# Two hybrid decoder layers on one core: the feed forward's low weight halves made by an accumulating transfer

## The chip, the core and the metric

The kernel runs on one core of a Trainium2 chip. The metric is device time in microseconds of one execution; lower is better. The kernel before takes 1782.17 us, the median of three runs (1781.2 to 1785.3).

## What is computed

Two post-norm decoder layers over 512 tokens of width 1024. Each merges three causal mixers (pooling, a state-space layer called S5, sparse attention) and ends with a squared-ReLU feed forward of width 4096. Only the last lines matter for the change:

```python
D_FF = 4 * D_MODEL
...
    x = layer_norm(ALPHA * x + merged @ w_out, ln1_g, ln1_b)
    h = jnp.square(jax.nn.relu(x @ w_ff1)) @ w_ff2
    return layer_norm(ALPHA * x + h, ln2_g, ln2_b)
```

`w_ff1` is 1024 x 4096 and `w_ff2` 4096 x 1024, in float32, for each of the two layers: 32 tiles of 128x1024 (512 KB) each, so 64 weight tiles a layer.

## The kernel before

**Split products.** Every matrix product is made of three on TensorE (PE) in the reduced format float32r. An operand x is split into hi (x rounded to float32r) and lo (x minus hi, again in float32r), and `mm3_` (L92 to L101) issues hi·hi (L98), hi·lo (L99) and lo·hi (L100) into one PSUM bank. In the first product of the feed forward the weights stand first, so their low half is read by L100 (`mm<-xh,wl`); in the second product they stand second, and it is read by L99 (`t<-wl,hi_a`).

**Loading a weight tile.** `wload` (L69 to L86) does it: a transfer on SyncE's queue (SP) brings 128x1024 float32 into a staging tile `wst` (L79, two buffers), ScalarE (ACT) rounds it into `wh` (L82, four buffers), and L85 subtracts to give `wl` (four buffers). The subtraction is on VectorE (DVE), or on GpSimd (POOL) where the tile comes from a pool of its own or `share` says so. A staging tile is free again when both of its readers, L82 and L85, are done, so SP's next load waits for them.

**The feed forward.** `feed_forward` (L1225) runs eight stages c. Stage c issues `up(c + 1)`, four tiles of the first weights, each used by 24 matmuls in a row, then `down(c)`, two halves of two tiles of the second weights. In a half four token blocks use both tiles, 48 matmuls. `up(0)` uses four tiles that were loaded in the stage before, and `down(7)` has code of its own. So in each layer 28 + 28 = 56 tiles go through the two calls that the change touches (L1100 and L1136).

**What else runs there.** In layer 0, POOL has other work during the feed forward: `ln_affine` (L215, lines L222 and L223, 16 instructions) applies scale and offset to the residual, and `s5_ahead` (L533) makes four sets of operands for the next layer's S5 (L461 to L464, L514 to L528, L542), which SP writes out (L547). At c = 2, `feed_forward` also loads four tiles of the next layer's input projection (L1249, `in_win`, tiles 1254 to 1265 in the rows of the order below), whose subtraction is on POOL. In layer 1, POOL has only `ln_affine`.

The tile framework sets the order of instructions on each engine when the program is built; each engine then takes its own in that order.

Of the kernel before, what the change touches and what calls it, by code (L numbers as in the profile page):

```python
# [12 lines left out]
AF = mybir.ActivationFunctionType  # L13
OP = mybir.AluOpType
# [12 lines left out]
class Kern:  # L27
# [38 lines left out]
        self.nc.scalar.activation(hi, src, AF.Copy, scale=scale)  # L66
        self.nc.vector.scalar_tensor_tensor(lo, src, scale, hi.bitcast(F32), op0=OP.mult, op1=OP.subtract)

    def wload(self, ap, pool=None):  # L69

        n = ap.shape[1]
        with ExitStack() as order:
            if self.held:
                self.held -= 1
                for ins in self.behind:
                    order.enter_context(self.tc.issue_after(ins))
            order.enter_context(self.tc.high_priority())
            st = self.t(self.wp, [128, n], F32, "wst", 2)
            self.loaded = self.nc.sync.dma_start(st, ap).ins  # L79
            wh = self.t(pool or self.wp, [128, n], R, "wh", 4)  # L80
            wl = self.t(pool or self.wp, [128, n], R, "wl", 4)
            self.nc.scalar.copy(wh, st)  # L82
            self.n_w += 1
            e = self.nc.gpsimd if pool or self.wpool or self.share and self.n_w % self.share == 0 else self.nc.vector
            e.tensor_tensor(wl, st, wh.bitcast(F32), OP.subtract)  # L85
        return wh, wl  # L86
# [1006 lines left out]
    def ffn(self, i, xs, p0):  # L1093

        nc, v = self.nc, self.nc.vector

        def up(c):
            hs = []
            for m in range(4):
                ps = p0[m] if c == 0 else self.xw([self.wload(self.A["wf1"][i, 4 * c + m])])[0]  # L1100
                h = self.t(self.mt, [128, 512], F32, "mt")
                nc.scalar.activation(h, ps, AF.Relu)  # L1102
                v.tensor_tensor(h, h, h, OP.mult)  # L1103
                hh, hl = self.pair("ab"[c % 2])
                self.hi_lo(hh, hl, h)
                hs.append((hh, hl))
            return hs

        def part(hs, ws, tb, half, c):
            ps = self.psum("mm" if c == 7 else "s" if tb % 2 else "t")  # L1110
            s = slice(tb * 128, (tb + 1) * 128)
            terms = []
            for k in range(4):
                hh, hl = hs[k]
                wh, wl = ws[2 * half + k // 2]
                cc = slice((k % 2) * 512, (k % 2 + 1) * 512)
                terms.append(((hh[:, s], hl[:, s]), (wh[:, cc], wl[:, cc])))
            self.mm3(ps, terms)
            r = xs[tb][:, half * 512:(half + 1) * 512]
            v.tensor_tensor(r, r, ps, OP.add)  # L1120

        def blocks(hs, ws, post):
            for tb in range(4):
                for half in range(2):
                    part(hs, ws, tb, half, 7)
                    if half:
                        post(tb)
                    yield

        def down(c, hs, post):  # L1130
            W = self.A["wf2"]
            if c < 7:
                for half in range(2):
                    ws = [None] * 4
                    for kp in range(2):
                        ws[2 * half + kp] = self.wload(W[i, c, half, kp])  # L1136
                    for tb in range(4):
                        part(hs, ws, tb, half, c)
            else:
                ws = [self.wload(W[i, c, half, kp]) for half in range(2) for kp in range(2)]  # L1140
                return blocks(hs, ws, post)

        return up, down

    def run(self):
# [214 lines left out]
```

## Time and profile before

| what | value |
|---|---|
| median of three runs | 1782.17 us |
| the profiled execution | 1785.11 us |
| its span, first to last instruction | 1783.3 us |
| PE busy | 94% of the span |
| DVE, ACT, POOL busy | 63%, 40%, 31% |
| HBM traffic over the span | 102 GB/s |

A profile row of a group gives line, engine, operation, tile out<-in, shapes and count, then busy time in us, mean ns of one, and idle time before it with what ended that. A row of a window gives each engine's busy time with its number of instructions, the granted clock of TensorE (1.00 is the higher of its two levels, 0.50 the lower), the share of the 16 transfer engines and GB/s.

### The profile page before, as it was taken

The numbers are of one execution on the slowest core, as the hardware profiler recorded it, in microseconds if no ns is written. First come the engines' busy times: TensorE is split into PE (matmuls) and PEld (weight loads), VectorE is DVE, ScalarE is ACT, GpSimd is POOL, SyncE is SP. The second block draws the span as 40 slices with busy tenths as digits, with TensorE's granted clock in tenths as the row PEclk, the third lists the DMA queues.
The fourth block names the chain that finished last, engine by engine and source line by source line (L and its number), as shares of the span: only waits on it lengthen the run. The fifth ranks groups of instructions, "written<-read, shape, count | busy, mean of one in ns | idle before, by whom it ended". The sixth has DMA issues, their size and how long they took to land.

```text
span 1783.3 us, 22543 instructions
## 1 busy us (share of the span) xinstructions
PE 1676.9 (94%) x8356; PEld 1402.0 (79%) x8356; DVE 1129.7 (63%) x2167; ACT 711.3 (40%) x1245; POOL 552.4 (31%) x640
## 2 busy tenths in 40 slices
PE   3959999999999998999998899999999999999996
PEld 2957887887779886888887788878787888888885
DVE  8797568676578654544476555866756784444447
ACT  2444336666534332233232433556664342332221
POOL 4993321322114999400024233132212060000002
PEclk9979999999999998999999999999999999999998
DMA  5313251111351243443316433311124133233331
GB/s 192 116 37 95 85 185 60 60 48 63 93 176 41 87 160 115 166 140 96 115 54 224 137 111 113 125 53 60 60 83 149 65 118 95 94 95 95 99 102 59
DMA packets 64334, 183.69 MB, mean 103 GB/s; under 512 B 12256, under 2 KB 21216, under 8 KB 63200
## 3 DMA queue, kind: packets, MB, share of 16 engines
q1 hardware_dynamic: 61632, 176.88, 30.5%
q10 hardware_dynamic: 2592, 5.38, 0.9%
q8 instruction: 65, 1.06, 0.2%
q14 instruction: 45, 0.37, 0.1%
HBM read 164.93 MB, written 17.30 MB: 102 GB/s over the span
## 4 chain that ended last, share of the span: by engine, by line
PE 71%; DVE 12%; POOL 10%; DMA 3%; ACT 2%; issue 1%; SPq 0%; DVEq 0%; ACTq 0%; POOLq 0%
PE mm L98 15%; PE mm L99 14%; PE mm L100 14%; PE s L99 3%; PE s L98 3%; PE s L100 3%; PE o L834 3%; PE t L98 2%; PE t L99 2%; PE t L100 2%; PE t L929 2%; DVE wl L85 1%; PE s L901 1%; ACT wh L82 1%; POOL ct L461 1%
## 5 line engine op out<-in xcount | busy, mean ns | idle before, releaser
L82 ACT CAST wh<-wst 128x1024 fp32r<-128x1024 f32 (+1 forms) x260 | 270.3, 1042 | 548.4 <-PE s L100 205.3
L85 DVE TENSOR_TENSOR wl<-wst,wh 128x1024 fp32r<-128x1024 f32 (+2 forms) x208 | 276.7, 1332 | 251.6 <-ACT wh L82 251.3
L98 PE MATMUL mm<-xh,wh 128*128 128x512 f32 (+1 forms) x1088 | 429.7, 395 | 6.1 <-ACT wh L82 4.9
L100 PE MATMUL mm<-xh,wl 128*128 128x512 f32 (+1 forms) x1088 | 419.3, 385 | 5.7 <-DVE wl L85 5.7
L99 PE MATMUL mm<-xl,wh 128*128 128x512 f32 (+1 forms) x1088 | 418.8, 385 | 0.0
L100 PEld LDWEIGHTS mm<-xh,wl 128*128 128x128 f32 x1088 | 205.1, 188 | 48.2 <-DVE wl L85 6.8
L98 PEld LDWEIGHTS mm<-xh,wh 128*128 128x128 f32 x1088 | 205.6, 189 | 44.5 <-ACT wh L82 5.4
L99 PEld LDWEIGHTS mm<-xl,wh 128*128 128x128 f32 x1088 | 205.9, 189 | 33.6
L85 POOL TENSOR_TENSOR wl<-wst,wh 128x1024 fp32r<-128x1024 f32 x52 | 132.1, 2543 | 243.1 <-ACT wh L82 243.0
L193 POOL TENSOR_TENSOR xm<-xm,ln_g 128x512 f32<-128x512 f32 x9 | 12.2, 1367 | 321.4 <-ACT xm L192 321.4
L906 ACT ACTIVATE P<-P,mx 128x512 f32<-128x512 f32 (+3 forms) x128 | 71.3, 558 | 62.7 <-DVE mx L904 62.3
L904 DVE CUSTOM_DVE_ANT_0 P<-s,mask 128x512 f32<-128x512 f32 (+3 forms) x128 | 59.6, 484 | 46.3 <-PE s L901 38.7
L62 DVE TENSOR_TENSOR Pl<-t,Ph 128x384 fp32r<-128x384 f32 (+1 forms) x96 | 57.3, 597 | 36.2 <-ACT Ph L61 36.0
L1120 DVE TENSOR_TENSOR xm<-xm,t 128x512 f32<-128x512 f32 x56 | 38.4, 686 | 56.0 <-PE t L100 53.2
L222 POOL TENSOR_TENSOR xm<-xm,hi_a 128x512 f32<-128x512 f32 x8 | 12.6, 1581 | 182.7 <-PE t L238 182.7
L222 POOL TENSOR_TENSOR xm<-xm,ln_g 128x512 f32<-128x512 f32 x16 | 30.1, 1884 | 121.8 <-PE t L238 121.8
L1103 DVE TENSOR_TENSOR mt<-mt 128x512 f32<-128x512 f32 x64 | 57.1, 892 | 14.8 <-ACT mt L1102 14.8
L1120 DVE TENSOR_TENSOR xm<-xm,s 128x512 f32<-128x512 f32 x56 | 38.2, 682 | 39.8 <-PE s L100 39.8
L913 POOL TENSOR_SCALAR P<-P,sm,gate 128x128 f32<-128x128 f32 x32 | 15.4, 480 | 153.1 <-DVE sm L908 153.1
L98 PE MATMUL t<-wh,hi_a 128*128 128x512 f32 x128 | 50.7, 396 | 8.9 <-ACT wh L82 8.9
L61 ACT CAST Ph<-t 128x384 fp32r<-128x384 f32 (+1 forms) x96 | 48.0, 505 | 26.9 <-PE t L929 26.8
L98 PE MATMUL mm<-hi_a,wh 128*128 128x512 f32 x132 | 54.9, 416 | 2.5 <-DVE lo_a L318 2.5
(406 smaller groups left out, 3839.8 us busy)
## 6 DMA issues: line engine op xcount, KB each, us to landing
wst<-in_wf_dram SPq DMA_DIRECT2D x128, 512.0 KB, 3.5
wst<-in_win_dram SPq DMA_DIRECT2D x80, 512.0 KB, 3.3
wst<-in_wup_dram SPq DMA_DIRECT2D x24, 512.0 KB, 3.5
wst<-in_wout_dram SPq DMA_DIRECT2D x16, 512.0 KB, 4.2
s5d<-zwe SPq DMA_DIRECT2D x4, 1664.0 KB, 8.6
zwe<-s5d SPq DMA_DIRECT2D x4, 1664.0 KB, 8.4
xd<-xm SPq DMA_DIRECT2D x8, 512.0 KB, 4.8
w<-in_w_dram SPq DMA_DIRECT2D x8, 512.0 KB, 7.4
```

What stands on the lines that cost most here:

```text
L61: a = self.nc.scalar.copy(hi, src)
L62: b = self.nc.vector.tensor_tensor(lo, src, hi.bitcast(F32), OP.subtract)
L82: self.nc.scalar.copy(wh, st)
L85: e.tensor_tensor(wl, st, wh.bitcast(F32), OP.subtract)
L98: mm(out, ah, bh, start=first and i == 0, stop=False, **kw)
L99: mm(out, ah, bl, start=False, stop=False, **kw)
L100: mm(out, al, bh, start=False, stop=last and i == n - 1, **kw)
L834: mm = lambda o, a, b, **k: nc.tensor.matmul(o, a, b, skip_group_check=True, **k)
L904: v.tensor_tensor_reduce(out=p, in0=ss[qb], in1=self.mask[:, 384 - 128 * qb:512], scale=-1.0, scalar=3e38, op0=OP.add, op1=OP.min, accum_o ...
L906: nc.scalar.activation(p, p, AF.Exp, bias=mx[:, qb:qb + 1], scale=-1.0, accum_out=c)
L1103: v.tensor_tensor(h, h, h, OP.mult)
L1120: v.tensor_tensor(r, r, ps, OP.add)
```

## The change

For the 112 tiles of the two calls, `wl` is no longer a subtraction. ACT writes the negative of the rounded tile into `wl` (a second pass over `wst`), and POOL's queue issues a transfer that reads the same 512 KB from HBM again and adds it to `wl` in place.

```diff
-    def wload(self, ap, pool=None):
+    def wload(self, ap, pool=None, sums=False):
...
             self.nc.scalar.copy(wh, st)
+            if sums:
+                self.nc.scalar.activation(wl, st, AF.Copy, scale=-1.0)
+                self.nc.gpsimd.dma_start(wl, ap, accum_op=OP.add)
+                return wh, wl
             self.n_w += 1
...
-                ps = p0[m] if c == 0 else self.xw([self.wload(self.A["wf1"][i, 4 * c + m])])[0]
+                ps = p0[m] if c == 0 else self.xw([self.wload(self.A["wf1"][i, 4 * c + m], sums=True)])[0]
...
-                        ws[2 * half + kp] = self.wload(W[i, c, half, kp])
+                        ws[2 * half + kp] = self.wload(W[i, c, half, kp], sums=True)
```

In the new program the lines from the old L83 on stand four lines lower: L226 is the old L222, L89 the old L85. L84 is ACT's negative and L85 POOL's transfer.

Three places of POOL's order show where the transfers went. First, the start of layer 0's feed forward, where `ln_affine` runs. `xm` is the residual, `ln_g` and `ln_b` scale and offset. Before:

```order
L222 TENSOR_TENSOR xm_982_4864<-xm_982_4864,ln_g_968_4836 128x512
L223 TENSOR_TENSOR xm_982_4864<-xm_982_4864,ln_b_969_4837 128x512
L222 TENSOR_TENSOR xm_982_4864<-xm_982_4864,ln_g_968_4836 128x512
L223 TENSOR_TENSOR xm_982_4864<-xm_982_4864,ln_b_969_4837 128x512
L222 TENSOR_TENSOR xm_983_4866<-xm_983_4866,ln_g_968_4836 128x512
```

Now:

```order
L226 TENSOR_TENSOR xm_982_4864<-xm_982_4864,ln_g_968_4836 128x512
L85 DMA wl_1072_5571<-in_wf1_dram 128x1024
L227 TENSOR_TENSOR xm_982_4864<-xm_982_4864,ln_b_969_4837 128x512
L226 TENSOR_TENSOR xm_982_4864<-xm_982_4864,ln_g_968_4836 128x512
L85 DMA wl_1079_5610<-in_wf1_dram 128x1024
L227 TENSOR_TENSOR xm_982_4864<-xm_982_4864,ln_b_969_4837 128x512
L226 TENSOR_TENSOR xm_983_4866<-xm_983_4866,ln_g_968_4836 128x512
L85 DMA wl_1086_5649<-in_wf1_dram 128x1024
L85 DMA wl_1093_5688<-in_wf1_dram 128x1024
```

Between the first transfer, wl_1072, and the last instruction of `s5_ahead` (just behind wl_1365) POOL's order now holds 33 transfers. The second place is POOL around the four tiles of the next layer's input projection, from the last of their subtractions on. Before:

```order
L85 TENSOR_TENSOR wl_1265_6511<-wst_1263_6508,wh_1264_6510 128x1024
L461 TENSOR_TENSOR et0_1331_6859<-zwe0_1146_6011,s5_pr_36_229 128x8x2
L462 TENSOR_TENSOR et1_1332_6860<-zwe0_1146_6011,s5_pi_37_230 128x8x2
L461 TENSOR_TENSOR ct0_1398_7200<-Zc_1392_7186,s5_are2_34_223 128x256
L462 TENSOR_TENSOR ct1_1399_7201<-Zc_1392_7186,s5_aim2_35_224 128x256
```

Now:

```order
L89 TENSOR_TENSOR wl_1265_6531<-wst_1263_6528,wh_1264_6530 128x1024
L465 TENSOR_TENSOR et0_1331_6887<-zwe0_1146_6023,s5_pr_36_229 128x8x2
L466 TENSOR_TENSOR et1_1332_6888<-zwe0_1146_6023,s5_pi_37_230 128x8x2
L467 TENSOR_TENSOR Wc_1316_6833<-ct0_1323_6853,ct1_1324_6854 128x4x16
L468 TENSOR_TENSOR Wc_1316_6833<-ct0_1323_6853,ct1_1324_6854 128x4x16
L85 DMA wl_1268_6537<-in_wf2_dram 128x1024
L467 TENSOR_TENSOR zwe0_1146_6023<-et0_1331_6887,et1_1332_6888 128x4x2
L468 TENSOR_TENSOR zwe0_1146_6023<-et0_1331_6887,et1_1332_6888 128x4x2
```

The low half of the next feed-forward tile, wl_1268, was DVE's and is now issued by POOL behind that subtraction and four instructions of `s5_ahead`. The third place is a little later, still POOL, where one set of S5 operands is written (L528, the old L524):

```order
L85 DMA wl_1281_6614<-in_wf2_dram 128x1024
L467 TENSOR_TENSOR Wc_1316_6833<-ct0_1327_6865,ct1_1328_6866 128x4x16
L468 TENSOR_TENSOR Wc_1316_6833<-ct0_1327_6865,ct1_1328_6866 128x4x16
L467 TENSOR_TENSOR zwe0_1146_6023<-et0_1335_6899,et1_1336_6900 128x4x8
L468 TENSOR_TENSOR zwe0_1146_6023<-et0_1335_6899,et1_1336_6900 128x4x8
L528 TENSOR_SCALAR zwe0_1146_6023<-Wc_1316_6833 64x20x16 x4
L465 TENSOR_TENSOR ct0_1394_7224<-bc_1391_7220,s5_kre_29_127 128x8x16
L466 TENSOR_TENSOR ct1_1395_7225<-bc_1391_7220,s5_kim_30_128 128x8x16
L465 TENSOR_TENSOR et0_1337_6905<-zwe0_1146_6023,s5_pr_36_229 128x8x16
L466 TENSOR_TENSOR et1_1338_6906<-zwe0_1146_6023,s5_pi_37_230 128x8x16
L85 DMA wl_1288_6677<-in_wf1_dram 128x1024
```

Between two neighbouring transfers there stand twelve instructions here, since L528 stands for four.

## Rows read from the trace of the kernel before

**Rows 1.** The page's busy time of each engine.
```profile
PE 1676.9 (94%) x8356; PEld 1402.0 (79%) x8356; DVE 1129.7 (63%) x2167; ACT 711.3 (40%) x1245; POOL 552.4 (31%) x640
```
**Rows 2.** Windows: stretch, length, each engine's busy us, granted clock, DMA share, GB/s.
```profile
560.00:905.00 345.00, 336.11 (x1524) 279.62 (x1523) 184.22 (x213) 103.80 (x131) 171.83 (x273) 0.99 0.38 122
...
1430.00:1740.00 310.00, 309.99 (x1410) 258.31 (x1409) 158.24 (x176) 94.24 (x121) 23.70 (x14) 1.00 0.32 101
...
1600.00:1700.00 100.00, 100.00 (x443) 82.77 (x442) 45.86 (x55) 27.88 (x34) 0.00 (x0) 1.00 0.30 95
```
**Rows 3.** Waits of PE in layer 0's feed forward, 556 to 910 us.
```profile
PE t L98 <- ACT wh L82: 8.9, 1, 8.9
```
**Rows 4.** Windows around that wait (same columns).
```profile
680.00:685.00 5.00, 2.45 (x11) 1.69 (x9) 0.15 (x1) 1.54 (x2) 4.73 (x9) 1.00 0.62 210
685.00:690.00 5.00, 0.00 (x0) 0.00 (x0) 2.98 (x2) 1.66 (x2) 5.00 (x6) 0.54 0.32 105
690.00:695.00 5.00, 3.67 (x9) 2.85 (x10) 3.00 (x3) 2.62 (x4) 5.00 (x10) 0.50 0.54 139
695.00:700.00 5.00, 5.00 (x22) 4.09 (x21) 2.95 (x3) 1.53 (x2) 5.00 (x11) 0.93 0.56 175
```
**Rows 5.** Timeline of POOL there: start us, us, instruction.
```profile
677.53 4.75 POOL L85 TENSOR_TENSOR wl<-wst,wh 128x1024 fp32r<-128x1024 f32 x2
...
684.39 2.35 POOL L85 TENSOR_TENSOR wl<-wst,wh 128x1024 fp32r<-128x1024 f32 x1 [0.27 <-ACT wh L82]
...
688.02 2.84 POOL L85 TENSOR_TENSOR wl<-wst,wh 128x1024 fp32r<-128x1024 f32 x1
```
**Rows 6.** Timeline of SP's queue there.
```profile
653.01 0.42 SPq L547 DMA_DIRECT2D s5d<-zwe  x1
662.92 19.72 SPq L79 DMA_DIRECT2D wst<-in_win_dram  x4
686.76 23.69 SPq L79 DMA_DIRECT2D wst<-in_wf_dram  x8
```
**Rows 7.** Timeline of ACT there.
```profile
690.23 1.05 ACT L82 CAST wh<-wst 128x1024 fp32r<-128x1024 f32 x1 [2.30 <-DMA wst<-in_wf_dram]
```
**Rows 8.** Groups of DVE and ACT in layer 1's feed forward, 1425 to 1750 us.
```profile
L85 DVE TENSOR_TENSOR wl<-wst,wh 128x1024 fp32r<-128x1024 f32 x60 | 78.7, 1314 | 87.2 <-ACT wh L82 87.2
L82 ACT CAST wh<-wst 128x1024 fp32r<-128x1024 f32 x60 | 63.1, 1053 | 164.4 <-PE s L100 106.1 <-PE mm L99 58.4
```
**Rows 9.** DMA issues of the page: tile, queue, count, size, us to landing.
```profile
wst<-in_wf_dram SPq DMA_DIRECT2D x128, 512.0 KB, 3.5
```
**Rows 10.** Timeline of ACT in layer 1, where no other engine but PE holds it.
```profile
1602.73 1.05 ACT L82 CAST wh<-wst 128x1024 fp32r<-128x1024 f32 x1 [6.18 <-PE s L100]
1604.09 1.06 ACT L82 CAST wh<-wst 128x1024 fp32r<-128x1024 f32 x1 [0.30 <-PE s L100]
1613.65 1.05 ACT L82 CAST wh<-wst 128x1024 fp32r<-128x1024 f32 x1 [8.51 <-PE s L100]
1615.01 1.05 ACT L82 CAST wh<-wst 128x1024 fp32r<-128x1024 f32 x1 [0.31 <-PE s L100]
```
**Rows 11.** Window of POOL's work in layer 0, and DVE's subtractions in it.
```profile
558.00:740.00 182.00, 173.11 (x813) 145.00 (x812) 104.10 (x102) 61.14 (x81) 172.02 (x273) 0.97 0.39 123
...
L85 DVE TENSOR_TENSOR wl<-wst,wh 128x1024 fp32r<-128x1024 f32 x32 | 48.6, 1521 | 35.3 <-ACT wh L82 35.3
```
**Rows 12.** Timeline of POOL in layer 0: one instruction short and long, and a set's write.
```profile
558.43 1.29 POOL L222 TENSOR_TENSOR xm<-xm,ln_g 128x512 f32<-128x512 f32 x1 [61.16 <-PE t L238]
...
566.81 2.15 POOL L223 TENSOR_TENSOR xm<-xm,ln_b 128x512 f32<-128x512 f32 x1
...
572.35 2.27 POOL L222 TENSOR_TENSOR xm<-xm,ln_g 128x512 f32<-128x512 f32 x1
...
615.64 5.21 POOL L524 TENSOR_SCALAR zwe<-Wc 64x320 f32<-64x320 f32 x4
```

## The prediction

> **What bounds the kernel now.** I read the busy times first: PE is busy 94% of the span and every other engine at most 63% [rows 1]. Then the windows, since the change touches only the two feed forwards. In layer 1's (1430 to 1740 us) PE is busy 309.99 of 310 us, in layer 0's (560 to 905) 336.11 of 345 [rows 2]. From 1600 to 1700 us there are 443 matmuls in 100 us, 0.226 us each, so a weight tile with its 24 matmuls lasts PE 5.42 us. That is the pace for all else: ACT, POOL and the transfer engines may each spend 5.42 us on a tile, no more. The waits of PE show one hole in both feed forwards: 8.9 us in layer 0, for a rounded tile from ACT [rows 3]. Behind it PE runs at the lower clock level: 9 matmuls fit into the 3.7 us up to 695, about 16 at the level of the other windows [rows 4]. With what is left of that after 695 the hole is worth about 11 us in all.
>
> The hole comes from POOL. The third and fourth loads of the next layer's projection need the staging tiles that POOL's subtractions free; POOL gets to these only at 677.5 us and ends the fourth at 690.9 [rows 5]. SP's next feed-forward load starts at 686.76, ACT rounds it at 690.23 [rows 6, 7].
>
> **What is removed.** 112 subtractions of 1.31 us on DVE, 147 us busy [rows 8]. The one wait of PE that is listed is not for them [rows 3], and DVE is busy half of layer 1's window [rows 2], so in itself this is worth nothing. It may help POOL in layer 0 (below).
>
> **What is added on ACT.** One more pass of 1.05 us a tile [rows 8], 59 us a layer. ACT is busy 94 of 310 us; with it, 153. Hidden, since ACT waits for PE before most of its roundings [rows 8].
>
> **What is added on the transfers.** A second 512 KB a tile. At 95 GB/s and a share of 0.30 [rows 2], a tile (5.52 us at that rate) takes 1.66 us of all 16 engines. No row shows an accumulating transfer. From below it costs what the plain load does, 1.66 us and 3.5 us to land [rows 9]. I bound it from above by three passes (reading the source, reading the old contents, writing apart), 4.98 us. I take two passes, 3.32 us, landing after 3.5 + 1.66 = 5.2 us, since two streams must be read and one is written. Load and accumulate then take 4.98 of 5.42 us, 92%; with the lower bound 61%, with the upper 122%. The Trainium skill's page "DMA: Bandwidth & Descriptors" says in "Rules for kernel authors" that an accumulate reads its destination and writes it later; no run here shows the price, and by that rule the sum would be the one with two passes rather than with the plain load.
>
> **Does it land in time?** Layer 1 has no POOL work after its first stage, so its rows show the lead. In a half, ACT rounds the two tiles at 1602.73 and 1604.09, the next two at 1613.65 and 1615.01 [rows 10]. The first pair is used from about 1615.0 on, when PE has finished the half between. With the new order on ACT (round, negative, round, negative) the negatives end at 1604.8 and 1606.9. POOL's issue is not in the trace either: the shortest comparable row is SP's 0.42 us, the longest POOL's own pass over such a tile, 2.35 us [rows 5, 6]; I take 1.0, their middle as a ratio. Then the transfers land at 1611.0 and 1613.1, 4.2 and 3.5 us before PE needs them (1615.2 and 1616.6). So layer 1 hides them. For now and then a load in the way of an accumulate I add **3 us**.
>
> **Layer 0 is different**, as POOL works from 558 to 740 us: 172.0 of 182 [rows 11]. Without the five instructions ahead of the first transfer (8.4 us, 558.4 to the start of the sixth at 566.8 [rows 12]) some 164 us are left for the stretch in which the new order holds 33 transfers. Three terms:
>
> 1. The hole. Its first part stays: the same four subtractions, the same loads. But wl_1268 is now issued by POOL. Rounding ends at 691.28 [rows 7], the negative at 692.33, the issue at 693.3, landing at 698.5. Before, a DVE subtraction of 1.4 us had it ready at 692.7. **+6 us**; with a plain landing +4.
> 2. POOL's pace. 33 tiles last PE 33 x 5.42 = 179 us. POOL needs 164 + 33 x 1.0 = 197 us, 18 more. Against that, POOL's instructions now stretch beside DVE: the same L222 takes 1.29 and 2.27 us [rows 12]. 32 subtractions leave that stretch [rows 11]; if each held POOL by half of its 1.31 us, that is 21 us back, and POOL is level with PE. I take the middle of level and 18, **+9 us**. Ends: 0, and with an issue of 2.35 us 18 + 33 x 1.35 = 63.
> 3. Bunching. The order puts whole groups between neighbouring transfers. Ahead of wl_1288 stand a write of a set, 5.2 us [rows 12], and eight small instructions of 0.2 to 0.7 us, near 3 us: 8.1 us, with the issue 9.1, which is 3.7 more than a tile's pace. The lead of 3.5 us would take one such group if POOL were otherwise early; level with PE it isn't. Four sets, four groups: **+15 us**; ends 0 and 15.
>
> What stands behind POOL's waits: each transfer waits there for ACT's negative, which waits for PE to free the buffer, so `s5_ahead` is held to PE's pace and ends later than 740 us. That costs nothing until 905, when the feed forward ends, and POOL is idle for 165 us before that now [rows 2, 11].
>
> **Sum**: 6 + 9 + 15 + 3 = +33 us on the profiled execution's 1785.1, so 1818. That execution lies 2.9 above the median of 1782.2; against the median, **1815 us**. With the cheap ends it is 4 us more than the median, with the dear issue some 85.
>
> **Rivals.**
>
> - *The transfers become the bound.* With three passes a tile takes 6.64 us of the engines, 1.22 over PE's pace; 112 times that is 137 us, and with term 1 143: 1925 us. With more (the transfer cut into many small pieces) it would be worse still, beyond my range. For it: two passes already make 92%, and the second reader of HBM meets the first. Against: nothing in the trace reads and writes in one transfer, so only the distance speaks. Sign: PE holes in layer 1 too, all the way to 1740 us. It decides from 3.76 us of the engines per accumulate (5.42 - 1.66).
> - *Hidden almost everywhere.* The accumulate lands like a load, POOL's relief is whole, the groups are absorbed by the lead: term 1 alone, +4, up to +14 with some bunching: 1786 to 1796.
> - *No change.* The same, with term 1 cancelled because POOL reaches the four subtractions a few microseconds sooner: within 3.6 us.
> - *Faster.* POOL, freed of DVE, ends the fourth subtraction 11 us sooner than 690.9; then the loads behind it come in time and the whole hole goes: 1782 - 11 = 1771 us. The new order also puts the first three of these subtractions ahead of the set's write. Against: the 20 or so transfers issued before it cost POOL about 20 us, as much as the relief of half a subtraction each. By the Trainium skill's page "SBUF — State Buffer", section "Who interferes with whom", a DVE instruction with two SBUF inputs and a GpSimd instruction that reads SBUF block each other wholly; by it each subtraction that goes could give back up to its full 1.31 us, and this rival's condition would be met if most of them hit. The two lengths of L222 agree with that rule, but not every subtraction falls on a POOL instruction that started later.
> - *It doesn't do what it says.* If POOL waited for an accumulate to land before its next instruction, it would lose 5 us a tile; then 33 x 5.2 = 172 us are added to its 164, 157 more than PE's 179, about 1940 us. Nothing in the rows speaks for it, and its time is that of the first rival.
>
> **How the numbers follow.** Slower by 15 to 85 us, my forecast: 0.54, since POOL's load in layer 0 is in the rows and only its overlap is open. Transfer-bound, or POOL held: 0.21. Hidden, +4 to +14: 0.14. No change: 0.06. Faster: 0.05. A measurement here tells 0.2%, 3.6 us, from no change. So faster 0.05, same 0.06, slower 0.89. The likeliest case lies between 1797 and 1867. The range from 1786 to 1940 takes in the hidden case and the bound of three passes; below it lie the same and faster cases (0.11), above it transfers dearer than three passes (about 0.09).
>
> **What the new profile would show.** Right: layer 1's window still full (PE within 3 us of 310), the new waits of PE all in layer 0, on `wl` from the transfer on POOL's queue, in groups at the sets' writes and longest near 690 to 730 us; accumulates landing 4 to 6 us after issue; `s5_ahead` ending after 780 us; POOL's L226 nearer 1.3 us than 1.9. Wrong: PE idle in layer 1, or a DMA share above 0.95 there (first rival); no hole near 690 us at all (faster); an issue on POOL well over 1 us would move term 2 alone.

## The result, and the profile after

The changed kernel takes **1792.49 us** (median of six, 1787.69 to 1798.9); the kernel before, run beside it on the same chip, 1782.6 (median of six, 1778.45 to 1785.47). The ratio is **1.0059, with a 95% interval of 1.0033 to 1.0084**: 9.9 us slower. I forecast slower, 1815 us, 33 us more. The sign was right, the size three times too large.

The profiled execution of the changed kernel is its longest, 1798.9 us with a span of 1797.1, so its shifts add up to 13.8 us (against the span of 1783.3 before) and not to 9.9. From its page, the busy times, the two new groups of instructions and the two transfers of a tile:

```profile
PE 1683.2 (94%) x8356; PEld 1403.7 (78%) x8356; DVE 1008.0 (56%) x2055; ACT 815.8 (45%) x1357; POOL 617.1 (34%) x752
...
L85 POOL DMA_DIRECT2D wl<-in_wf_dram x112 | 100.7, 910 | 351.7 <-ACT wl L84 350.9
...
L84 ACT ACTIVATE wl<-wst 128x1024 fp32r<-128x1024 f32 x112 | 118.0, 1055 | 155.4 <-PE s L103 150.8
...
wst<-in_wf_dram SPq DMA_DIRECT2D x128, 512.0 KB, 5.7
wl<-in_wf_dram POOLq DMA_DIRECT2D x112, 512.0 KB, 7.8
```

Against [rows 1] DVE is freed of 122 us, ACT has 105 more, POOL 65. An issue is 0.91 us long on POOL, an accumulate lands 7.8 us after it (median), and the plain load, 3.5 us before [rows 9], now takes 5.7. Windows of the changed kernel, with the columns of [rows 2], the last one around the first new wait:

```profile
560.00:910.00 350.00, 335.23 (x1505) 276.87 (x1504) 121.22 (x146) 155.52 (x188) 193.28 (x329) 0.98 0.81 204
1440.00:1750.00 310.00, 307.48 (x1387) 255.47 (x1386) 92.70 (x118) 145.61 (x176) 66.38 (x69) 0.99 0.84 194
1600.00:1700.00 100.00, 100.00 (x443) 82.81 (x442) 26.52 (x39) 46.93 (x57) 15.70 (x18) 1.00 0.85 195
...
598.00:608.00 10.00, 8.14 (x29) 6.41 (x29) 4.54 (x6) 1.98 (x3) 9.49 (x25) 0.83 0.96 242
```

From 1600 to 1700 us PE still does 443 matmuls in 100 us, with the transfer engines at 0.85: the change costs nothing in this steady stretch. What it costs stands in five waits, PE's timeline in the changed kernel (the last bracket is the wait and what ended it):

```profile
600.02 0.50 PE L103 MATMUL t<-wl,hi_a 128*128 128x512 f32 x1 [1.86 <-DMA wl<-in_wf_dram]
...
691.10 0.79 PE L102 MATMUL t<-wh,hi_a 128*128 128x512 f32 x1 [4.62 <-ACT wh L82]
699.90 0.79 PE L103 MATMUL t<-wl,hi_a 128*128 128x512 f32 x1 [6.73 <-DMA wl<-in_wf_dram]
...
747.81 0.50 PE L103 MATMUL t<-wl,hi_b 128*128 128x512 f32 x1 [1.57 <-DMA wl<-in_wf_dram]
...
1476.95 0.50 PE L103 MATMUL t<-wl,hi_a 128*128 128x512 f32 x1 [2.51 <-DMA wl<-in_wf_dram]
```

They are 17.3 us long; the one wait of before was 8.9 [rows 3]. Each new one is for the low half of a second weight, in the hi·lo matmul. A wait costs more than its length: in the 10 us from 598 on, with 1.86 us of waiting, the granted clock is 0.83, and 29 matmuls fit where the same stretch of the kernel before had 46:

```profile
598.00:608.00 10.00, 10.00 (x46) 8.29 (x45) 7.45 (x9) 3.70 (x5) 9.72 (x23) 1.00 0.24 83
```

So the wait near 690 us begins at 686.5 instead of 682.4. With the same matmul looked up in both traces, PE falls behind the kernel before by 4.0 us at the first wait, 3.2 at the hole, 2.1 near 746 us and 4.7 near 1474 us. Between them it keeps step, 4.0 us behind at 605 and at 682 us, 9.3 at 755 and 9.6 at 915. So these places make up the 13.8 us.

### The profile page after: what moved, and what is told of

Its sections match the earlier page's. It is cut to its first block, busy times and chain, and to the rows that moved or that the text cites. A ratio compares the mean times of both kernels' runs of the same rounds, so it can differ in the third digit from the quotient of the medians.

```text
span 1797.1 us, 22712 instructions
## 1 busy us (share of the span) xinstructions
PE 1683.2 (94%) x8356; PEld 1403.7 (78%) x8356; DVE 1008.0 (56%) x2055; ACT 815.8 (45%) x1357; POOL 617.1 (34%) x752
## 4 chain that ended last, share of the span: by engine, by line
PE 71%; DVE 13%; DMA 6%; POOL 5%; ACT 3%; issue 2%; SPq 0%; ACTq 0%; DVEq 0%; POOLq 0%
PE mm L102 14%; PE mm L103 14%; PE mm L104 14%; PE s L103 3%; PE s L104 3%; PE s L102 3%; PE o L838 3%; PE t L103 3%; PE t L104 3%; PE t L102 3%; PE t L933 2%; DMA wl<-in_wf_dram 2%; DMA wst<-in_wf_dram 1%; DVE wl L89 1%; ACT wh L82 1%
## 5 line engine op out<-in xcount | busy, mean ns | idle before, releaser
L85 POOL DMA_DIRECT2D wl<-in_wf_dram x112 | 100.7, 910 | 351.7 <-ACT wl L84 350.9
L89 POOL TENSOR_TENSOR wl<-wst,wh 128x1024 fp32r<-128x1024 f32 x52 | 131.6, 2533 | 245.8 <-ACT wh L82 245.7
L1107 DVE TENSOR_TENSOR mt<-mt 128x512 f32<-128x512 f32 x64 | 67.0, 1049 | 221.6 <-ACT mt L1106 221.6
L84 ACT ACTIVATE wl<-wst 128x1024 fp32r<-128x1024 f32 x112 | 118.0, 1055 | 155.4 <-PE s L103 150.8
L89 DVE TENSOR_TENSOR wl<-wst,wh 128x1024 fp32r<-128x1024 f32 (+2 forms) x96 | 126.0, 1314 | 90.5 <-ACT wh L82 90.1
L226 POOL TENSOR_TENSOR xm<-xm,ln_g 128x512 f32<-128x512 f32 x16 | 26.5, 1656 | 123.0 <-PE t L242 123.0
L103 PE MATMUL t<-wl,hi_a 128*128 128x512 f32 x128 | 51.5, 402 | 11.1 <-DMA wl<-in_wf_dram 11.1
```

Of the source, the lines that this page charges most:

```text
L84: self.nc.scalar.activation(wl, st, AF.Copy, scale=-1.0)
L85: self.nc.gpsimd.dma_start(wl, ap, accum_op=OP.add)
L103: mm(out, ah, bl, start=False, stop=False, **kw)
```

## The experiments

All medians below stand beside runs of the kernel before on the same chip, taken together with them (medians of 1781.92 to 1784.03 us); a ratio is to those.

### Which of the two calls costs

**Up only**: `sums` is left out of the call for the second weights.

```diff
-                        ws[2 * half + kp] = self.wload(W[i, c, half, kp], sums=True)
+                        ws[2 * half + kp] = self.wload(W[i, c, half, kp])
```

> Only the 56 tiles of the first weights take the new way, the 56 of the second weights are subtracted on DVE as before. Theory (late landing at a few places): all four new waits of PE in the changed kernel are for wl in halves of the second product, so nothing is lost here, and the hole near 690 us is at most as long as before's 8.9 us: 1776 to 1784 us, 0 to -6 against the kernel before. Rival (the load on the transfer engines, spread over all tiles): half of the tiles cost half, +4 to +6, 1787 to 1789 us. Rival (POOL's pace, my terms 2 and 3): half of the issues, so less than half of the cost, +2 to +5.

Measured: 1778.66 us, ratio 0.9975 (0.9965 to 0.9986), 4.5 us *faster* than before. The hole near 690 us is gone; two short waits for `wl` in the first product (2.7 and 1.4 us, layer 0) are new. Both rivals fall. The theory's time came out, its reason only in part: a transfer in the first product can land late too.

**Down only**: `sums` is left out of the call for the first weights.

```diff
-                ps = p0[m] if c == 0 else self.xw([self.wload(self.A["wf1"][i, 4 * c + m], sums=True)])[0]
+                ps = p0[m] if c == 0 else self.xw([self.wload(self.A["wf1"][i, 4 * c + m])])[0]
```

> The other half: only the 56 tiles of the second weights take the new way. Theory (late landing at a few places): every wait stays, so the time is the changed kernel's, +8 to +11 us against the kernel before, 1790 to 1794 us; PE waits for wl near 598, 690 and 1474 us as before. Rival (load on the transfer engines): landings fall from 7.8 us towards 5 us with half of the accumulates, the waits near 598 and 1474 us (1.9 and 2.5 us) close, and the time is +3 to +6 us.

Measured: 1803.08 us, ratio 1.0112 (1.0095 to 1.0128). The waits stay, as the theory said, but the cost doubles to 20 us, which neither expected: half of the transfers is dearer than all of them. DVE's timeline, PE's and a piece of POOL's in this kernel:

```profile
710.97 9.89 DVE L89 TENSOR_TENSOR wl<-wst,wh 128x1024 fp32r<-128x1024 f32 x1 [14.26 <-ACT wh L82]
```
```profile
720.91 0.80 PE L104 MATMUL mm<-xh,wl 128*128 128x512 f32 x1 [5.90 <-DVE wl L89]
```
```profile
711.00 0.86 POOL L465 TENSOR_TENSOR et<-zwe,s_pr 128x256 f32<-128x256 f32 x1
711.58 0.85 POOL L466 TENSOR_TENSOR et<-zwe,s_pi 128x256 f32<-128x256 f32 x1
...
719.03 0.46 POOL L467 TENSOR_TENSOR Wc<-ct,ct 128x64 f32<-128x64 f32 x1
719.31 0.46 POOL L468 TENSOR_TENSOR Wc<-ct,ct 128x64 f32<-128x64 f32 x1
```

A subtraction that takes 1.3 us elsewhere [rows 8] took 9.89 while POOL ran through 16 small instructions without a gap, the last of them done at 719.8, and PE waited 5.9 us for it. By the matched matmuls PE is 10.0 us behind the kernel before ahead of this wait and 18.9 behind it. So in this mix a DVE subtraction seems to be held by POOL's S5 work. The test is to take that work off POOL, **down only with the S5 operands on DVE** (two further edits, shown below under POOL's queue):

> The run with only the second weights' tiles by transfer (20 us slower than the kernel before), and the operands of s5_ahead made on DVE. Theory (its extra 10 us against the changed kernel come from DVE's subtractions and POOL's run of small instructions holding each other up: a subtraction of 9.9 us, and the first transfer issued 3.6 us later than in the changed kernel): both go, and the time is that of the changed kernel or less, 1786 to 1794 us. Rival (the transfers of the second weights are late for their own sake, so that nothing on POOL matters): 1799 us or more.

Measured: 1795.28 us, ratio 1.0063 (1.0049 to 1.0078), the changed kernel's ratio within the intervals. The subtractions in layer 0 (min, median and max in ns), with the work on POOL and with it on DVE:

```profile
L89 DVE TENSOR_TENSOR wl<-wst,wh x32: 1210/1225/9889, 563.6 to 910.0; 128x1024 fp32r<-128x1024 f32 x32
```
```profile
L89 DVE TENSOR_TENSOR wl<-wst,wh x32: 1210/1224/2322, 562.4 to 896.7; 128x1024 fp32r<-128x1024 f32 x32
```

The longest is 2.3 us now, PE's wait for DVE is gone, and 8.7 of the 19.9 us with it, as the theory has it. The edit also shortens POOL's queue, so it doesn't tell the two effects apart everywhere: the wait near 598 us, which isn't for DVE, costs 4.4 us here instead of 8.0.

### What is lost to the transfers, and what is won without them

**Negative only**: the transfer is taken out.

```diff
                 self.nc.scalar.activation(wl, st, AF.Copy, scale=-1.0)
-                self.nc.gpsimd.dma_start(wl, ap, accum_op=OP.add)
                 return wh, wl
```

> The transfer is left out, so wl holds only the negative of the rounded weights and the products lack the part that the transfer would add. ACT's second pass stays, DVE's subtractions are gone, POOL issues nothing. Theory (ACT's pass is hidden, all of the loss is the transfers landing late; the rounding part of the hole near 690 us stays 4.6 us where it was 8.9): 1774 to 1780 us, 3 to 8 us less than the kernel before. Rival (ACT's second pass itself delays the rounding of tiles at the start of a stage): waits for ACT near 598 and 1474 us, 1784 us or more. Rival (the relief of POOL from DVE is nothing): the hole is 8.9 us again, 1782 us.

Measured: 1771.88 us, ratio 0.9938 (0.9926 to 0.9951), 11.3 us faster; better than my theory, since the hole is not shortened but gone. No wait of PE over 0.6 us is left in either feed forward. Its window over the stretch of [rows 11]:

```profile
558.00:740.00 182.00, 181.69 (x857) 152.21 (x856) 62.66 (x75) 95.99 (x118) 148.71 (x274) 1.00 0.40 129
```

POOL does the same work in 148.71 us instead of 172.02 [rows 11], 23.3 us less. POOL's last of the four subtractions ends at 682.0 us, 8.9 sooner than before (690.9). So ACT's pass is hidden, the relief of POOL is real and is worth 11 us, and the transfers cost those 11 and 9.9 more.

**Plain**: the same transfers overwrite instead of adding.

```diff
-                self.nc.gpsimd.dma_start(wl, ap, accum_op=OP.add)
+                self.nc.gpsimd.dma_start(wl, ap)
```

> POOL issues the same 112 transfers at the same places, but each overwrites wl instead of adding to it, so the low half then holds the whole weight and the products are others. The issue on POOL, its waits for ACT and the traffic from HBM stay; only the adding goes. The rows of the changed kernel give 2.98 us of 16 engines for an accumulate and 1.66 for a load. Theory A (the adding is what is dear: accumulates follow one another and land 7 to 9 us after issue): landing near 3.5 to 5 us, the waits for wl near 598, 746 and 1474 us go, 1772 to 1780 us. Rival B (POOL's queue: the transfers and the waits for ACT hold up POOL's other work, so that the fourth subtraction for the input projection ends near 692 us, as in the changed kernel, where it ends at 682 us without any transfer): the hole near 690 us stays at 8 us or more in all, 1783 to 1791 us.

Measured: 1781.77 us, ratio 1.0003 (0.9991 to 1.0015). Of its page the issue and the transfer, and PE's waits in layer 0:

```profile
L85 POOL DMA_DIRECT2D wl<-in_wf_dram x112 | 61.7, 551 | 374.3 <-ACT wl L84 373.8
...
wl<-in_wf_dram POOLq DMA_DIRECT2D x112, 512.0 KB, 4.8
```
```profile
PE t L103 <- DMA wl<-in_wf_dram: 5.5, 1, 5.5
PE t L102 <- ACT wh L82: 4.6, 1, 4.6
```

Each theory is right about its own place. The waits near 598, 746 and 1474 us go once the transfer lands in 4.8 instead of 7.8 us: those are the price of the adding, some 10 us between the two ratios (4.0 + 2.1 + 4.7 in the changed kernel's trace). The hole near 690 us stays, 10.1 us in its two parts, so the adding is not what makes it: with transfers on its queue, plain or not, POOL ends the four subtractions later than without them, at 686.6 us here and at 692.1 in the changed kernel.

### The hole near 690 us

**Before, with the input projection's four tiles on DVE**, and no transfer at all:

```diff
-                w0 = [self.wload(A["win"][i + 1, j], w0p) for j in range(4)]
+                w0 = [self.wload(A["win"][i + 1, j], w0p, dve=True) for j in range(4)]
...
-            e = self.nc.gpsimd if pool or self.wpool or self.share and self.n_w % self.share == 0 else self.nc.vector
+            e = self.nc.gpsimd if pool and not dve or self.wpool or self.share and self.n_w % self.share == 0 else self.nc.vector
```

> The kernel before, with one edit: the four tiles of the next layer's input projection in layer 0's feed forward are subtracted on DVE, not on POOL; no transfer is added. Theory (the 8.9 us hole near 690 us is made by POOL coming late to these four): the hole goes, and the time is that of the kernel without transfers, 1770 to 1774 us. Rival (the four loads simply stand between two feed-forward loads on SP's queue, whoever subtracts): a hole of 3 us or more stays, 1776 to 1782 us.

Measured: **1771.92 us, ratio 0.9938 (0.9925 to 0.995)**: the hole is POOL's four late subtractions, as the prediction read it, and moving them beats both kernels. From 560 to 910 us PE is full:

```profile
560.00:910.00 350.00, 349.40 (x1630) 292.63 (x1630) 200.88 (x266) 112.22 (x150) 166.29 (x268) 1.00 0.38 120
```

**The changed kernel with the same edit** (`dve=True` in the call, the same line for the engine):

> The changed kernel with the same edit as in the run before: the four input projection tiles subtracted on DVE. Theory (the hole near 690 us is in both kernels POOL coming late to these four, and the transfer wl_1268 behind them): both parts of it (4.6 and 6.7 us) go, what is left are the waits near 598, 746 and 1474 us (4.0 + 2.1 + 4.7 us): 1778 to 1784 us. Rival (the transfer of wl_1268 lands late whoever subtracts): a wait of 5 us or more for wl near 690 us stays, 1785 to 1790 us.

Measured: 1785.65 us, ratio 1.0020 (1.0004 to 1.0036). The waiting for the rounded tile goes, the waiting for the transfer does not; the rival holds. ACT, POOL and PE in this kernel:

```profile
683.57 1.05 ACT L82 CAST wh<-wst 128x1024 fp32r<-128x1024 f32 x1 [2.09 <-DMA wst<-in_wf_dram]
```
```profile
685.99 0.89 POOL L85 DMA_DIRECT2D wl<-in_wf_dram  x1 [1.44 <-ACT wl L84]
```
```profile
693.52 0.79 PE L103 MATMUL t<-wl,hi_a 128*128 128x512 f32 x1 [7.64 <-DMA wl<-in_wf_dram]
```

The tile is rounded at 684.6, in time for PE; its low half is there at 693.5. The way of an accumulate from the end of the rounding (negative, wait, issue, landing) is 8.9 us, that of a DVE subtraction 1.6 (before: rounded at 691.28 [rows 7], subtracted by 692.86):

```profile
691.31 1.55 DVE L85 TENSOR_TENSOR wl<-wst,wh 128x1024 fp32r<-128x1024 f32 x1 [2.65 <-ACT wh L82]
```

**The two tiles behind them on DVE as well**:

```diff
-                        ws[2 * half + kp] = self.wload(W[i, c, half, kp], sums=True)
+                        ws[2 * half + kp] = self.wload(W[i, c, half, kp], sums=not (i < DEPTH - 1 and c == 2 and half == 0))
```

> The changed kernel with the input projection's four tiles subtracted on DVE, and with them the two tiles of the second weights that follow on SP's queue (layer 0, c = 2, first half). Theory (from the end of a tile's rounding an accumulate takes some 9 us, a subtraction on DVE 1.3; at 686 us the lead is short, which the four extra loads cause): the wait of 7.6 us there goes too, what is left are 598 and 1466 us: 1778 to 1782 us. Rival (plain loads, landing in 5.5 us beside accumulates where they took 3.5, bring the rounding itself late): a wait of 2 us or more for wh near 685 us, 1783 to 1788 us.

Measured: 1786.07 us, ratio 1.0015 (1.0002 to 1.0027). The time is the rival's, its wait is not: the wait moves one half on, 4.0 us at 695 us, again for `wl`. Here POOL has its part: it issues that transfer at 693.7, 5.7 us after the negative, behind the write of a set that ends at 692.2.

**Six tiles on DVE**, also those of the first half of c = 0 in both layers:

```diff
-                        ws[2 * half + kp] = self.wload(W[i, c, half, kp], sums=not (i < DEPTH - 1 and c == 2 and half == 0))
+                        ws[2 * half + kp] = self.wload(W[i, c, half, kp], sums=half > 0 or c != 0 and (c != 2 or i == DEPTH - 1))
```

> The run before, and the first half of c = 0 in both layers is subtracted on DVE too, so 106 of 112 tiles keep the new way. Theory (the other 106 cost nothing, as their lead is longer than the way of an accumulate): no PE wait for wl or wh in either feed forward, and the time is that of the kernel without transfers, 1770 to 1775 us. Rival (as when the whole first stage was taken back: the scheduler then puts POOL's first transfer behind a long group of the operands for S5, and a wait of 6 us or more comes back at the next half): 1778 us or more.

Measured: 1779.92 us, ratio 0.9982 (0.9971 to 0.9993). The waits near 598 and in layer 1 go. The one at 695 us stays, 4.2 us, and one of 1.4 near 661 us is new. POOL comes late to the transfers for 695 us, as the rival has it; its timeline in this kernel:

```profile
684.19 5.19 POOL L528 TENSOR_SCALAR zwe<-Wc 64x320 f32<-64x320 f32 x4
...
691.14 1.83 POOL L85 DMA_DIRECT2D wl<-in_wf_dram  x2
```

The negative for the first of these two transfers ends at 688.66, the issue starts 2.5 us later. My claim that the other 106 tiles cost nothing falls: 8 us remain against the kernel without transfers. Is it POOL, or the way of the accumulate? **The six tiles, and the S5 operands on DVE**:

> The run with six tiles on DVE, and the operands of s5_ahead made on DVE too, so that POOL has nothing between its transfers. Theory (the wait of 4.2 us that is left near 695 us comes from POOL's write of a set, 5.2 us, ahead of the transfer, and no tile outside the six has too short a lead): that wait goes, and the time is that of the kernel without transfers, 1770 to 1775 us. Rival (the accumulate's way of 8.9 us is too long for the next half as well, whoever stands ahead of it): a wait of 2 us or more for wl near 695 us, 1777 to 1781 us.

Measured: 1781.09 us, ratio 0.9984 (0.9973 to 0.9994), no gain. PE's waits in layer 0 now:

```profile
PE t L103 <- DMA wl<-in_wf_dram: 3.1, 2, 2.2
PE t L102 <- ACT wh L82: 1.2, 1, 1.2
PE t L103 <- DVE wl L89: 0.8, 1, 0.8
```

The wait at 697 us is halved to 2.2, small ones of up to 1.2 us come in its place, and the time stays. The rival's wait is there: POOL stands idle until ACT's negative for that half and issues 0.4 us after it, and the way to `wl` is still too long. But the waits for the rounded tile and for DVE's subtraction are new with the S5 work on DVE, so this run gives back part of what it takes off POOL.

### POOL's queue

**The S5 operands on DVE**: `s5_ahead`'s products and copies leave POOL, in the changed kernel.

```diff
-        nc, gl = self.nc, self.nc.gpsimd
+        nc, gl = self.nc, self.nc.vector if alone else self.nc.gpsimd
...
-                        self.s5_operands(pool, i, r, qs[r % 2], self.nc.gpsimd, True)
+                        self.s5_operands(pool, i, r, qs[r % 2], self.nc.vector, True)
```

> The changed kernel with the operands of s5_ahead made on DVE instead of POOL; POOL keeps the transfers, the scale and offset, the cleared tiles and the four subtractions. Theory B (POOL's queue in layer 0 is what makes the transfers late, by its other work standing between them): no PE wait for wl in layer 0 after 600 us, the hole near 690 us goes, 1776 to 1784 us, if DVE's longer queue makes no wait of its own. Rival A (the landing of an accumulate, 7 to 9 us, is too long by itself): waits for wl in layer 0 stay near 598 and 746 us, 1786 us or more.

Measured: 1792.29 us, ratio 1.0058 (1.0045 to 1.0072), the changed kernel's own time. Nothing is won. The profiled execution is the shortest of the six, 1782.8 us where the others took 1790.5 to 1794.5, so it doesn't show where the median comes from. In it the wait near 746 us is gone, the one near 598 is 1.9 us, and the hole is there in both parts. ACT, PE and POOL:

```profile
683.89 0.62 ACT L61 CAST hi_b<-mt 128x512 fp32r<-128x512 f32 x1 [6.39 <-DVE mt L1107]
```
```profile
686.94 0.79 PE L102 MATMUL t<-wh,hi_a 128*128 128x512 f32 x1 [4.19 <-ACT wh L82]
...
696.70 0.79 PE L103 MATMUL t<-wl,hi_a 128*128 128x512 f32 x1 [7.69 <-DMA wl<-in_wf_dram]
```
```profile
688.25 0.88 POOL L85 DMA_DIRECT2D wl<-in_wf_dram  x1 [0.36 <-ACT wl L84]
```

The first part decides nothing, since DVE's longer queue makes a wait of its own, which theory B had excepted: ACT stands 6.4 us behind DVE's L1107 before it rounds the fourth of the four tiles. The second part speaks against theory B: POOL issues `wl`'s transfer 0.4 us after the negative, with nothing else in its way, and PE still waits 7.7 us.

Whether POOL is late in the changed kernel itself, that kernel's trace tells. These are the negatives of the four tiles whose low halves PE waits for, and POOL's issues of their transfers:

```profile
590.16 1.05 ACT L84 ACTIVATE wl<-wst 128x1024 fp32r<-128x1024 f32 x1
...
690.96 1.05 ACT L84 ACTIVATE wl<-wst 128x1024 fp32r<-128x1024 f32 x1
...
734.31 1.06 ACT L84 ACTIVATE wl<-wst 128x1024 fp32r<-128x1024 f32 x1
...
1464.06 1.05 ACT L84 ACTIVATE wl<-wst 128x1024 fp32r<-128x1024 f32 x1
```
```profile
592.21 0.89 POOL L85 DMA_DIRECT2D wl<-in_wf_dram  x1
...
693.36 0.87 POOL L85 DMA_DIRECT2D wl<-in_wf_dram  x1
...
735.78 1.05 POOL L85 DMA_DIRECT2D wl<-in_wf_dram  x1
...
1465.52 0.89 POOL L85 DMA_DIRECT2D wl<-in_wf_dram  x1 [1.55 <-ACT wl L84]
```

The issue starts 1.0, 1.4, 0.4 and 0.4 us after the negative ends; the landing takes 7.8, 6.5, 12.0 and 11.4 us more. So these low halves are late by the landing and not by POOL's queue, and theory B falls for the order that the change has. POOL's S5 work shows in one of them: the two transfers ahead of that of 735.78 were issued 6.9 and 3.4 us after their negatives, so three started within 4.4 us, and they landed after 7.9, 9.9 and 12.0 us. Over the whole stretch from 558 to 760 us POOL still waits for ACT (total, times, longest):

```profile
POOL wl L85 <- ACT wl L84: 16.1, 11, 2.7
```

**No transfers in the first stage** (`up(1)` and `down(0)` subtract on DVE):

```diff
-                ps = p0[m] if c == 0 else self.xw([self.wload(self.A["wf1"][i, 4 * c + m], sums=True)])[0]
+                ps = p0[m] if c == 0 else self.xw([self.wload(self.A["wf1"][i, 4 * c + m], sums=c > 1)])[0]
...
-                        ws[2 * half + kp] = self.wload(W[i, c, half, kp], sums=True)
+                        ws[2 * half + kp] = self.wload(W[i, c, half, kp], sums=c > 0)
```

> The first stage's tiles (the four of up(1) and the four of down(0)) are subtracted on DVE, the others take the new way. Theory (the waits near 598 and 1474 us belong to that stage, where ACT and POOL reach the tile late): both go, and their 4.0 and 4.7 us with them; the hole near 690 us stays: 1782 to 1786 us. Rival (the stage only happens to be the first; the same lateness shows up one stage later): the waits move to c = 1 and the time stays at 1790 to 1793 us.

Measured: 1803.83 us, ratio 1.0119 (1.0104 to 1.0135), worse than both. The waits near 598 and 1474 us go, but the scheduler now places POOL's first transfer behind a whole run of S5 work. ACT, POOL and PE in this kernel:

```profile
603.64 1.06 ACT L84 ACTIVATE wl<-wst 128x1024 fp32r<-128x1024 f32 x1 [2.98 <-PE s L103]
```
```profile
612.46 4.24 POOL L528 TENSOR_SCALAR zwe<-Wc 64x320 f32<-64x320 f32 x4
...
617.48 1.03 POOL L85 DMA_DIRECT2D wl<-in_wf_dram  x1
```
```profile
623.35 0.79 PE L104 MATMUL mm<-xh,wl 128*128 128x512 f32 x1 [6.38 <-DMA wl<-in_wf_dram]
```

The negative ends at 604.7, the transfer is issued 12.8 us later, and PE waits 6.4 us. This is the bunching of my third term, in an order that has it; near 697 us a second wait of 12.7 us follows.

### Layer 1 alone

**Only layer 1**, and **the same with the loads of scale and offset three stages later**:

```diff
-                ps = p0[m] if c == 0 else self.xw([self.wload(self.A["wf1"][i, 4 * c + m], sums=True)])[0]
+                ps = p0[m] if c == 0 else self.xw([self.wload(self.A["wf1"][i, 4 * c + m], sums=i == DEPTH - 1)])[0]
...
-                        ws[2 * half + kp] = self.wload(W[i, c, half, kp], sums=True)
+                        ws[2 * half + kp] = self.wload(W[i, c, half, kp], sums=i == DEPTH - 1)
```

> Only layer 1's 56 tiles take the new way; layer 0 is that of the kernel before, with its hole of 8.9 us. Theory (the waits are independent of one another, each where a tile's lead is shorter than the way of an accumulate): layer 1 keeps its one wait near 1460 us, +2 to +5 us against the kernel before, 1784 to 1787 us, and no other wait follows up to 1740 us. Rival (the transfer engines, busy 0.85 there, make the loss all along): more than +6 us.

> The run before, and the two broadcast loads of scale and offset that ACT's queue issues at the start of layer 1's feed forward (512 KB each, in the stretch where an accumulate took 11.4 us to land) are issued three stages later. Theory A (those two loads stretch the accumulates of the first stage): the wait near 1460 us goes and the time is that of the kernel before, within 2 us, 1780 to 1784 us. Theory B (the stage's first tiles are rounded late by ACT, whose queue stands in front of them): the wait stays at 1.5 us or more and the time at +2 to +5 us.

Measured: 1785.13 us, ratio 1.0009 (0.9998 to 1.0020), and 1784.70, ratio 1.0003 (0.999 to 1.0016). PE's waits in layer 1, first kernel and second:

```profile
PE t L103 <- DMA wl<-in_wf_dram: 3.5, 1, 3.5
```
```profile
PE t L103 <- DMA wl<-in_wf_dram: 0.6, 1, 0.6
```

One wait at the start and none after, as expected, for 2.1 us by the medians, with no change at all still inside the interval. The later loads shorten that wait in the profile from 3.5 to 0.6 us and the landings of the three accumulates before it from at most 10.0 to at most 8.3 us; the two times can't be told apart.

## Why the prediction was right or wrong

**What bounds the kernel; what is removed; ACT.** Right. PE stays at 100% from 1600 to 1700 us, and the negative-only run shows the second ACT pass wholly hidden.

**The transfers.** The two passes were right: the share rose from 0.30 [rows 2] to 0.85, so an accumulate takes 0.55 x 5.42 = 2.98 us of the engines where I had 3.32; the plain second stream took (0.57 - 0.30) x 5.42 = 1.5 us by its window from 1600 to 1700 us. So the transfers are not the bound, and that rival fell. The Trainium skill's page "DMA: Bandwidth & Descriptors", section "Rules for kernel authors", says that an accumulate reads its destination and writes it later, and the 2.98 against 1.5 us agree with that. **The landing was wrong**: 7.8 us, not 5.2. I took the landing of a load and added one pass, as if an accumulate found the engines free. In the changed kernel a pair issued at 1617.71 and 1619.61 us landed after 7.3 and 9.2 us, and the four that PE waits for after 6.5 to 12.0.

**Does it land in time?** In the steady state yes, though the margins of 4.2 and 3.5 us were thin. At the start of a feed forward it does not, and the prediction names neither start. For layer 1 it has +3 in all, for "a load in the way"; the wait near 1474 us is 2.5 us long and costs 4.7. The same place in layer 0, the first half of c = 0, has no term: 4.0 us.

**Term 1, the hole.** Mechanism right, +6 against 3.2. The low half's way came out almost as written, issued at 693.36 us (forecast 693.3) and there at 699.9 (698.5). It cost less because PE reaches the hole 4.0 us late, so the wait for the rounded tile shrinks from 8.9 to 4.6 us while one of 6.7 follows.

**Term 2, POOL's pace, +9: the step that failed first.** The relief was sized rightly, by a guess of one half that came out (21 against 23.3 measured). By my own sum that left POOL level with PE; I then took the middle between level and 18 us late. It was the low end: POOL waits 11 times for ACT, `s5_ahead` ends at 759.7 us and not after 780, and between the waits PE keeps step with the kernel before.

**Term 3, bunching, +15: the step that failed most.** It needed POOL to be level or late in every set. In the change's order one wait of 1.57 us, near 746 us, can be put down to it, worth 2.1. The runs without transfers in the first stage and with the tiles around the projection on DVE show that the mechanism exists, transfers issued 12.8, 5.7 and 2.5 us late, in other orders; I had read the groups from the order and put all four at full price.

**In sum.** Terms 2 and 3 held 24 of my 33 us and were worth some 2; what the runs show in their place is the landing, 2.6 us longer than I had it in the median, at the two starts (4.0 + 4.7 us, where I had 3) and at the hole (3.2). Of the trace's 13.8 us my terms saw 5.3, the hole and the wait near 746 us, so more than half came from the starts, which I did not see: that the sign came out as clearly as it did is part luck. The time is the one of the rival "hidden almost everywhere", 1786 to 1796, but not by its mechanism, in which the accumulate lands like a load. The rival "faster" had its mechanism right as well: without the transfers the hole goes and the time is 1771.9, where I put 1771. It failed by what I held against it, since the transfers on POOL's queue use up the relief and the fourth subtraction ends at 692.1 us, and by the change's own 8.9 us way to `wl`. The Trainium skill's page "SBUF — State Buffer", section "Who interferes with whom", says that a DVE instruction with two SBUF inputs contends with a GpSimd instruction that reads SBUF. POOL's 23.3 us and DVE's 9.89 us subtraction agree with that.

**What stays open.** With the six tiles back on DVE and POOL's S5 work gone, 8 us remain against the kernel without transfers. They lie in one place: against the kernel before with its four tiles on DVE, PE is 0.8 us behind up to 680 us, 7.6 at 705 and 8.9 from 735 us to the end of the feed forward. The waits listed are 5.1 of that, and most of the rest is the lower clock behind them, 16 matmuls in 5 us where the other kernel has 24:

```profile
685.00:690.00 5.00, 5.00 (x16) 3.94 (x17) 4.39 (x8) 2.54 (x4) 0.00 (x0) 0.67 0.69 203
```

How much of it is the transfers' and how much is DVE's longer queue, no run separates. And whether the later loads of scale and offset gain anything in layer 1 is below what the runs can tell.

## What to carry to other kernels

Price an asynchronous replacement by its whole way from ready input to ready output, and set that against the lead of each tile where the lead is shortest (the start of a stage, extra loads in the same buffers), not against throughput: here transfer engines 85% busy cost nothing from 1600 to 1700 us, and a way of 8.9 us cost what was lost. Before a queue is called the bound, compare when each input was ready with when the queue took it: at the four waits here that was at most 1.4 us, and the landing 6.5 to 12.0. And look first at the wait that is already there: moving four subtractions to the engine with time gave 10 us, more than any version of the change.

## What the runs showed of the hardware that I had not expected

- An accumulating transfer of 512 KB has an issue of 0.91 us on POOL, a plain one of the same shape 0.55; it lands after 7.8 us, the plain one after 4.8 (medians).
- A second stream slows the first: the plain load landed in 3.5 us without it, 4.0 beside plain transfers and 5.7 beside accumulates (medians).
- A DVE subtraction with two inputs in SBUF, 1.3 us elsewhere, took 9.89 us beside a run of 16 POOL instructions without gaps. The run with half of the transfers was 10 us slower than the one with all, until POOL's work was taken off it.
